# Reversing the queries of a tile in a sparse-attention trunk, so that the relative bias is read from a table of 24 KB

## The chip, the cores and the metric

The kernel runs on one core of one Trainium2 chip. The metric is device time in microseconds (us) of one execution; the time of a kernel is the median of its runs. The core has five engines with queues of their own: TensorE (PE in the profile; its weight loads are PEld), VectorE (DVE), ScalarE (ACT), GpSimd (POOL) and SyncE (SP). SP, ACT and POOL can issue DMAs, which 16 DMA engines carry out.

## The reference, cut to what matters

Two layers work on 256 tokens of width 2048. The first layer projects the normed input into a recurrence branch and an attention branch. The attention has 16 query heads and 4 key heads of width 128, and an indexer that scores every (query, key) pair and leaves 64 keys per query. What the change touches is this part:

```python
def block(bi):                      # 128 queries at a time
    s_h = jax.nn.relu(jnp.einsum('bqhd,bsd->bqhs', iqb, ik))
    score = jnp.einsum('bqhs,bqh->bqs', s_h, iwb) * idx_scale
    score = jnp.where(admissible[None], score, -jnp.inf)   # key < limit(query), chunks of 64
    _, sel = lax.top_k(score, topk)
    ...
    logits = jnp.einsum('bqgrd,bqkgd->bqgrk', qg, kg) * att_scale
    bias = rel_table[t5_bucket(sel - q_pos[None, :, None])]   # depends on key - query alone
    probs = jax.nn.softmax(logits + bias, axis=-1)
    o = jnp.einsum('bqgrk,bqkgd->bqgrd', probs, vg)
```

The bias of a head is a function of key position minus query position. Everything else (norms, gates, recurrence, the second layer's gated MLP, the embedding that is added after each layer) is matrix products with large weights, and elementwise work between them.

## The kernel before, in words

**The weight stream.** All large weights are float32 in HBM. They come as chunks of 128 x 1024 numbers (512 KB; the indexer's are 128 x 736) in one long list, `self.chunks`. For each chunk SP loads `raw` (13 buffers; L147), ACT rounds it to `hi` (L155), DVE subtracts to get `lo` (L156), and PE multiplies `hi` by the high and the low part of the activations and `lo` by the high part (three fp32r matmuls of 512 columns each: L189 to L191 into `pg`, or L229 to L231 into `Z`, `V`, `U`). Splits run three chunks ahead of their matmuls, loads up to five more ahead of the splits. Some chunks are made by adding a second weight block onto a used `raw` with a DMA that POOL issues (L160).

**Background tasks.** Everything else is generators (`idx_task`, `q_task`, `head_pair`, ...). After each chunk's matmuls the main loop takes one step of each live generator, so that a `yield` means about one chunk. A scheduler then puts the instructions of each engine into their final order; each engine runs its own list in that order, and waits where an operand is not there yet.

**The bias before.** `bias_table` computes a 16 x 384 table `bt` (head by key minus query) with one matmul (L487). An ACT-issued DMA (L493) then writes 128 copies of each head's row into the HBM tile `bias_d`, copy q shifted by q elements. For each pair of heads a POOL-issued DMA (L695) reads `bias`, a 128 x 2 x 256 tile whose row for query q is a piece of copy q.

**The attention before.** The transposes on PE have the data as weights and `ident` as the moving operand: of `iq` (L443, tile `iqt`), of `q` (L443, tile `qt`), and of the exponentials `L` (L735, tile `pt`). `head_pair` makes `bm` = bias + mask on POOL (L702, L703), the logits `lg` on PE (L706, L707), `L` = lg * rq + bm on DVE (L717) with its row maximum (L719), the exponentials and their sums `sm` on ACT (L725), then the reciprocal of the sums on DVE (L729, L731), the transposes `pt`, their copy `PT` on ACT (L737), the products with v (L744 to L746), and the scaled output `yb` on DVE (L754). `rq`, the norm of the queries, comes from the sums of squares `ss` (L630) by L675 on DVE and a power on POOL (L676). There are 8 head pairs, 4 query groups and 4 indexer steps.

**DMA lanes.** The DMAs that SP and ACT issue take eight completion semaphores in turn; an issue waits until the DMA that last had its semaphore has landed.

Of the kernel before, what the change touches and what calls it, by code (L numbers as in the profile page):

```python
# [27 lines left out]
T = 256  # L28
# [3 lines left out]
H = 16  # L32
# [49 lines left out]
class Trunk:  # L82
# [351 lines left out]
            nc.vector.tensor_tensor(lo, src, hi.bitcast(F32), op=OP.subtract)  # L434
        return hi, lo

    def fm(self, a0, a1, name="fm"):

        pt = self.pa(name)
        with self.tc.issue_after(self.last_mm.ins):  # L440
            for k in range(2):
                for t, x in ((0, a0), (1, a1)):
                    self.nc.tensor.transpose(pt[:, k * T + t * 128:k * T + (t + 1) * 128],  # L443
                                             x[:, k * 128:(k + 1) * 128], self.ident)
        return pt.rearrange("p (a b) -> p a b", a=2)

    def rms(self, ss, key):
# [18 lines left out]
    def consts(self):  # L466
        nc, a = self.nc, self.a
        self.cols = self.kept([128, C_ALL], "cols")
        nc.sync.dma_start(self.cols, a["cols"])
        self.ident = self.kept([128, 128], "ident")  # L470
        nc.gpsimd.dma_start(self.ident, a["ident"])
        self.mhalf = self.kept([128, 8], "mhalf")
        nc.gpsimd.memset(self.mhalf, -0.5)
        warm = self.kept([128, 8], "warm")
        nc.scalar.activation(warm, self.mhalf, AF.Tanh)
        self.r = {}

    def bias_table(self):
        nc, a = self.nc, self.a
        rel = self.kept([32, H], "rel")  # L480
        nc.gpsimd.dma_start(rel, a["rel_bias"])
        oh = self.kept([32, N_BUCKET_COLS], "oh")
        nc.gpsimd.dma_start(oh, a["onehot"])
# [4 lines left out]
        sb = self.kept([H, N_BUCKET_COLS], "bt")  # L488
        nc.scalar.activation(sb, ps[:H, :N_BUCKET_COLS], AF.Copy)

        bd = self.bias_d = self.dram.tile([H, 128, 512], F32, name="bias_d")
        yield
        nc.scalar.dma_start(bass.AP(tensor=bd.tensor, offset=bd.offset, ap=[[128 * 512, H], [513, 128], [1, 383]]),  # L493
                            sb[:, None, :383].to_broadcast([H, 128, 383]))
        self.done.add("bias")

    def lru_params(self):
# [28 lines left out]
    def idx_task(self, i, ps):  # L526

        nc = self.nc
        cp = lambda o, x: nc.scalar.activation(o, x, AF.Copy)
        if i == 0:  # L530
            self.iq = [[self.t(name="iq") for _ in range(2)] for _ in range(2)]
            self.iw = self.kept([128, 2, IH], "iw")
            self.score = self.t([128, 384], name="score")
            ikd = [self.t([128, 128], name="ikd") for _ in range(2)]
            for t in range(2):
                cp(ikd[t][:, 0:64], ps[t][:, 0:64])
                nc.vector.tensor_scalar(self.iw[:, t], ps[t][:, 64:80], IDX_SCALE, None, op0=OP.mult)
# [24 lines left out]
        yield  # L562

    def iq_task(self, j):

        nc = self.nc
        yield from self.until(f"iq{j // 2}")
        o = (j % 2) * T
        pt = self.fm(self.iq[j // 2][0][:, o:o + T], self.iq[j // 2][1][:, o:o + T], "iqt")
        iq = self.t([128, 2, T], name="iqT")  # L570
        nc.scalar.activation(iq, pt, AF.Copy)
        yield
        rl = []
        for step in range(3):
            for h, r in rl:
                hh = j * 4 + h
                for (c0, c1, t) in ((0, 256, 1), (256, 384, 0)):
                    w = self.iw[:, t, hh:hh + 1]
                    if hh == 0:
                        nc.vector.tensor_scalar(self.score[:, c0:c1], r[:, c0:c1], w, None, op0=OP.mult)  # L580
                    else:
                        nc.vector.scalar_tensor_tensor(self.score[:, c0:c1], r[:, c0:c1], w,
                                                       self.score[:, c0:c1], op0=OP.mult, op1=OP.add)
            rl = []
            if step < 2:
                ps = [self.pa("sc") for _ in range(2)]
                for c0, c1, q0 in ((0, 256, 128), (256, 384, 0)):
                    for b in (0, 64):
                        nc.tensor.matmul(ps[b // 64][:, c0:c1], iq[b:b + 64, step, q0:q0 + 128],
                                         self.ik[b:b + 64, 0:c1 - c0], start=True, stop=True)  # L590
                for i in range(2):
                    r = self.t([128, 384], name="rl")
                    nc.scalar.activation(r, ps[i][:, :384], AF.Relu)
                    rl.append((2 * step + i, r))
            if step == 1 and j < 3:
                self.spawn(self.iq_task(j + 1))
            yield 2
        if j == 3:
            yield from self.topk()

    def topk(self):
        nc = self.nc
        sc = self.score
        nc.vector.memset(sc[0:64, 192:256], OUT_OF_RANGE)
        nc.vector.memset(sc[0:64, 320:384], OUT_OF_RANGE)
        for rnd in range(8):
            for c0, c1 in ((0, 256), (256, 384)):
                m8 = self.sm([128, 8])
# [59 lines left out]
    def q_task(self, g, ps):  # L668
# [7 lines left out]
        nc.gpsimd.tensor_tensor(self.flat(rq), self.flat(rq), self.mhalf, op=OP.pow)  # L676
        self.rq[g] = rq
        qT = []
        for p in range(2):
            pt = self.fm(qs[0][:, p * T:(p + 1) * T], qs[1][:, p * T:(p + 1) * T], "qt")  # L680
# [3 lines left out]
        yield  # L684
        yield from self.until("mask", "k", "v", "bias")
        for p in range(2):
            self.spawn(self.head_pair(g, p, qT[p]), 0)
# [2 lines left out]
    def head_pair(self, g, p, qT):  # L690
# [39 lines left out]
        for i, t in ((0, 1), (1, 0)):  # L730
            nc.vector.tensor_scalar(rc[:, 2 * i:2 * i + 2], rc[:, 2 * i:2 * i + 2], self.rth("x", t), None, op0=OP.mult)  # L731
        for h in range(2):
            pt = self.pa("pt")
            for o, c in ((0, 256), (128, 0), (256, 128)):
                nc.tensor.transpose(pt[:, o:o + 128], L[h][:, c:c + 128], self.ident)  # L735
            x = self.t([128, 384], name="PT")
            nc.scalar.activation(x, pt[:, :384], AF.Copy)  # L737
            PT.append(x)
        yield
        po = self.pa("o")  # L740
        kv = slice(g * 128, (g + 1) * 128)
# [500 lines left out]
def _layout(i):  # L1242
# [28 lines left out]
    def plain(key, w):  # L1271
# [35 lines left out]
        "ident": np.eye(128, dtype=np.float32),  # L1307
        "onehot": _buckets(),
    }

# [14 lines left out]
```

## Time and profile before

| | us |
|---|---|
| median of 3 runs (1245.07 to 1247.82) | 1246.75 |
| the profiled execution, its own time | 1248.01 |
| its span from first to last instruction | 1246.2 |
| PE busy, share of the span | 1227.4 (98%) |
| DVE busy | 944.3 (76%) |
| ACT busy | 785.0 (63%) |
| POOL busy | 147.4 (12%) |

The profiled execution took 1.26 us more than the median, and 1.8 us of its time lie outside the span. A matmul's record includes its way through the array, so that records overlap: the time a matmul costs the stream is the distance of its start to the next one's, which the chain view gives directly.

### The profile page before, as it was taken

How to read it: one execution, taken by the hardware profiler on the slowest of the kernel's cores; microseconds unless marked ns; L12 is line 12 of the kernel's file. 1: busy time of each engine (PE TensorE's matmuls, PEld its weight loads, DVE VectorE, ACT ScalarE, POOL GpSimd, SP SyncE). 2: the span in 40 equal slices, each digit the busy share in tenths (PEclk: the TensorE clock that was granted, in tenths of full speed). 3: DMA queues.
4: the chain of work that ended last, by engine and by line, in shares of the span. 5: the costliest groups of instructions: out<-in, count | busy, mean ns of one | idle time of the engine just before them, and what ended most of it. 6: DMA issues, size and time to landing. Idle time of an engine off the chain costs nothing.

```text
span 1246.2 us, 16543 instructions
## 1 busy us (share of the span) xinstructions
PE 1227.4 (98%) x5780; PEld 1023.8 (82%) x5780; DVE 944.3 (76%) x1487; ACT 785.0 (63%) x1099; POOL 147.4 (12%) x178
## 2 busy tenths in 40 slices
PE   7999999999999999999999999999999999999998
PEld 7978887888888888888888888788888888887886
DVE  6779658786677778775568877887899778677865
ACT  6755546664477878863466776676765656565753
POOL 0001131412000001000110110032112000100100
PEclk9999999999999999999999999999999999999999
DMA  9997997636546555576787798889999965986961
GB/s 345 253 249 231 299 219 240 227 128 199 183 157 201 172 186 177 178 239 216 188 246 250 187 291 281 225 241 271 274 274 277 279 222 156 244 267 203 261 186 43
DMA packets 82868, 279.31 MB, mean 224 GB/s; under 512 B 9264, under 2 KB 11968, under 8 KB 82784
## 3 DMA queue, kind: packets, MB, share of 16 engines
q1 hardware_dynamic: 66672, 225.18, 52.0%
q0 software_dynamic: 14048, 49.94, 21.2%
q10 hardware_dynamic: 2064, 3.14, 1.9%
q8 instruction: 45, 0.74, 0.2%
q14 instruction: 39, 0.32, 0.1%
HBM read 270.89 MB, written 7.33 MB: 223 GB/s over the span
## 4 chain that ended last, share of the span: by engine, by line
PE 89%; DMA 5%; DVE 3%; issue 2%; ACT 1%; SPq 0%; POOL 0%; DVEq 0%; ACTq 0%
PE pg L191 22%; PE pg L189 22%; PE pg L190 22%; DMA bias_d<-bt 3%; PE U L229 1%; PE U L231 1%; PE U L230 1%; DVE lo L156 1%; ACT hi L155 1%; PE ht L443 1%; PE Z L230 1%; PE Z L229 1%; PE Z L231 1%; PE V L230 1%; PE U L290 1%
## 5 line engine op out<-in xcount | busy, mean ns | idle before, releaser
L156 DVE TENSOR_TENSOR lo<-raw,hi 128x1024 fp32r<-128x1024 f32 (+1 forms) x492 | 587.6, 1212 | 201.5 <-ACT hi L155 197.2
L155 ACT ACTIVATE hi<-raw 128x1024 fp32r<-128x1024 f32 (+1 forms) x492 | 511.5, 1048 | 350.2 <-PE pg L191 256.0
L189 PE MATMUL pg<-hi,xh 128*128 128x512 f32 (+1 forms) x1376 | 536.9, 390 | 6.8 <-ACT xh L426 6.3
L190 PE MATMUL pg<-lo,xh 128*128 128x512 f32 (+1 forms) x1376 | 532.0, 387 | 0.5 <-DVE lo L156 0.5
L191 PE MATMUL pg<-hi,xl 128*128 128x512 f32 (+1 forms) x1376 | 531.9, 387 | 0.5 <-DVE xl L427 0.4
L189 PEld LDWEIGHTS pg<-hi,xh 128*128 128x128 f32 x1376 | 259.5, 189 | 57.6 <-ACT xh L426 6.9
L191 PEld LDWEIGHTS pg<-hi,xl 128*128 128x128 f32 x1376 | 259.0, 188 | 51.7 <-DVE xl L427 1.6
L190 PEld LDWEIGHTS pg<-lo,xh 128*128 128x128 f32 x1376 | 259.5, 189 | 49.1 <-DVE lo L156 1.0
L160 POOL DMA_DIRECT2D raw<-in_w7h x32 | 27.7, 866 | 357.3 <-DMA raw<-in_w 197.5
L160 POOL DMA_DIRECT2D raw<-in_w x48 | 41.8, 892 | 203.7 <-DVE lo L156 110.6
L426 ACT ACTIVATE xh<-ht,cols 128x256 fp32r<-128x256 f32 x48 | 22.0, 469 | 19.1 <-DVE xl L427 11.9
L803 POOL TENSOR_TENSOR tt<-tt,tg 128x512 f32<-128x512 f32 x8 | 10.3, 1294 | 183.1 <-ACT tt L801 164.3
L229 PE MATMUL U<-hi,xh 128*128 128x512 f32 x72 | 29.0, 403 | 0.0
L231 PE MATMUL U<-lo,xh 128*128 128x512 f32 x72 | 28.1, 390 | 0.0
L230 PE MATMUL U<-hi,xl 128*128 128x512 f32 x72 | 28.1, 390 | 0.0
L427 DVE SCALAR_TENSOR_TENSOR xl<-ht,cols,xh 128x256 fp32r<-128x256 f32 x48 | 22.6, 481 | 5.7 <-ACT xh L426 5.6
L725 ACT ACTIVATE L<-L,s 128x256 f32<-128x256 f32 (+1 forms) x32 | 14.3, 448 | 15.5 <-DVE s L719 14.8
L434 DVE TENSOR_TENSOR xl<-s,xh 128x512 fp32r<-128x512 f32 x32 | 22.0, 687 | 1.9 <-ACT xh L433 1.9
L433 ACT ACTIVATE xh<-s 128x512 fp32r<-128x512 f32 x32 | 19.9, 622 | 4.8 <-DVE s L414 4.7
L717 DVE SCALAR_TENSOR_TENSOR L<-lg,rq,bm 128x256 f32<-128x256 f32 (+1 forms) x32 | 12.0, 410 | 14.4 <-POOL bm L702 12.4
L829 DVE SCALAR_TENSOR_TENSOR xc<-xat,cols,xc 128x255 f32<-128x255 f32 (+2 forms) x48 | 22.2, 477 | 0.5
L231 PE MATMUL V<-lo,xh 128*128 128x512 f32 x48 | 18.8, 391 | 0.5 <-DVE lo L156 0.5
(310 smaller groups left out, 1346.9 us busy)
## 6 DMA issues: line engine op xcount, KB each, us to landing
raw<-in_w SPq DMA_DIRECT2D x356, 512.0 KB, 5.0
raw<-in_w POOLq DMA_DIRECT2D x48, 512.0 KB, 8.7
raw<-in_w7h POOLq DMA_DIRECT2D x32, 512.0 KB, 7.1
raw<-in_w7h SPq DMA_DIRECT2D x24, 512.0 KB, 4.4
raw<-in_idx_w SPq DMA_DIRECT2D x24, 368.0 KB, 7.4
raw<-in_pe_w SPq DMA_DIRECT2D x8, 512.0 KB, 6.0
bias_d<-bt ACTq DMA_DIRECT2D x1, 3064.0 KB, 35.9
x<-in_xT SPq DMA_DIRECT2D x8, 256.0 KB, 7.3
```

The costliest lines, as they stand in the source:

```text
L155: nc.scalar.activation(hi[:, :c.cols], raw, AF.Copy)
L156: self.last_lo = nc.vector.tensor_tensor(lo[:, :c.cols], raw, hi[:, :c.cols].bitcast(F32), op=OP.subtract)
L160: nc.gpsimd.dma_start(c.raw, c.next.ap, accum_op=OP.add)
L189: self.nc.tensor.matmul(ps, xh, wh, start=(c == order[0] and k == 0), stop=False)
L190: self.nc.tensor.matmul(ps, xh, wl, start=False, stop=False)
L191: self.last_mm = self.nc.tensor.matmul(ps, xl, wh, start=False, stop=(c == order[-1] and k == 1))
L229: nc.tensor.matmul(st[b], ah, wh, start=new and k == 0, stop=False, skip_group_check=True)
L230: nc.tensor.matmul(st[b], al, wh, start=False, stop=False, skip_group_check=True)
L231: self.last_mm = nc.tensor.matmul(st[b], ah, wl, start=False, stop=(c == order[3] and k == 1), skip_group_check=True)
L426: nc.scalar.activation(hi[:, s], src[:, s], AF.Copy, scale=g)
L427: nc.vector.scalar_tensor_tensor(lo[:, s], src[:, s], g, hi[:, s].bitcast(F32), op0=OP.mult, op1=OP.subtract)
L829: nc.vector.scalar_tensor_tensor(xc[:, s, k:], xa[:, s, :T - k], col(C_CW + (3 - k) * 16 + f), xc[:, s, k:], op0=OP.mult, op1=OP.add)
```

## The change

Within each tile of 128 queries, the queries are taken in reverse for the logits and the scores. The bias row of the query in partition i then starts i elements further on in the table than that of partition 0, so a read with a step of one element per partition takes it straight from `bt`. `bias_d` becomes that table (16 x 384 floats, 24 KB) and its write is one row per head. To reverse the queries, the transposes of `iq`, `q` and `L` become matmuls with `flip`, the reversed identity, as the moving operand (the one for `L` turns the order back). What is held per query in partitions is reversed by small matmuls with `flip` as weights: `iw` (128 x 32, once, then an ACT copy), `ss` (128 x 8, once per query group) and `sm` (128 x 4, once per head pair, into a free part of the second `pt`). The steps behind these follow them: `rq` is computed one step later, and the reciprocal reads `pt` after the transposes. The constant `ident` grows from 64 to 128 KB.

```diff
-    def fm(self, a0, a1, name="fm"):
+    def fm(self, a0, a1, name="fm", flip=False):
...
+                    if flip:
+                        self.nc.tensor.matmul(o, x, self.flip, start=True, stop=True)
+                    else:
+                        self.nc.tensor.transpose(o, x, self.ident)
...
-        bd = self.bias_d = self.dram.tile([H, 128, 512], F32, name="bias_d")
-        yield
-        nc.scalar.dma_start(bass.AP(tensor=bd.tensor, offset=bd.offset, ap=[[128 * 512, H], [513, 128], [1, 383]]),
-                            sb[:, None, :383].to_broadcast([H, 128, 383]))
+        self.bias_d = self.dram.tile([H, N_BUCKET_COLS], F32, name="bias_d")
+        yield
+        nc.scalar.dma_start(self.bias_d, sb)
...
+                nc.tensor.matmul(pt[:, T:T + 2 * IH], self.flip, self.flat(self.iw), start=True, stop=True)
+            self.iw = self.kept([128, 2, IH], "iwf")
+            nc.scalar.activation(self.flat(self.iw), pt[:, T:T + 2 * IH], AF.Copy)
...
-        rq = self.kept([128, 2, 4], "rq")
-        nc.vector.tensor_scalar(rq, ss, 128 * EPS, None, op0=OP.add)
...
+        ps = self.pa("rq")
+        with self.tc.issue_after(self.last_mm.ins):
+            nc.tensor.matmul(ps[:, 0:8], self.flip, self.flat(ss), start=True, stop=True)
+        rq = self.kept([128, 2, 4], "rq")
+        nc.vector.tensor_scalar(self.flat(rq), ps[:, 0:8], 128 * EPS, None, op0=OP.add)
...
-        nc.gpsimd.dma_start(bt, bass.AP(tensor=bd.tensor, offset=bd.offset + h0 * 128 * 512 + 127,
-                                        ap=[[512, 128], [128 * 512, 2], [1, T]]))
+        nc.gpsimd.dma_start(bt, bass.AP(tensor=bd.tensor, offset=bd.offset + h0 * N_BUCKET_COLS,
+                                        ap=[[1, 128], [N_BUCKET_COLS, 2], [1, T]]))
...
-        rc = self.sm([128, 4])
-        nc.vector.reciprocal(rc, sm)
...
-                nc.tensor.transpose(pt[:, o:o + 128], L[h][:, c:c + 128], self.ident)
+                nc.tensor.matmul(pt[:, o:o + 128], L[h][:, c:c + 128], self.flip, start=True, stop=True)
+            if h == 1:
+                nc.tensor.matmul(pt[:, 384:388], self.flip, sm, start=True, stop=True)
...
+        rc = self.sm([128, 4])
+        nc.vector.reciprocal(rc, pt[:, 384:388])
```

SP's list keeps its order. On DVE the reciprocal of a head pair moves behind several splits (`lo`). This is the first pair; `s_1725` and `s_1730` are its sums `sm`. Before:

```order
L717 SCALAR_TENSOR_TENSOR L_1743<-lg_1689,rq_1599,bm_1686 128x128
L719 TENSOR_REDUCE s_1724<-L_1743 128x1
L156 TENSOR_TENSOR lo_1751<-raw_1221,hi_1750 128x1024
L729 RECIPROCAL s_1802<-s_1725 128x4
L731 TENSOR_SCALAR s_1802<-s_1802,rx_466 128x2 x2
L156 TENSOR_TENSOR lo_1774<-raw_1661,hi_1773 128x1024
```

With the change, on DVE at the same place:

```order
L156 TENSOR_TENSOR lo_1756<-raw_1224,hi_1755 128x1024
L156 TENSOR_TENSOR lo_1779<-raw_1666,hi_1778 128x1024
L156 TENSOR_TENSOR lo_1791<-raw_1697,hi_1790 128x1024
L156 TENSOR_TENSOR lo_1829<-raw_1710,hi_1828 128x1024
L156 TENSOR_TENSOR lo_1860<-raw_1736,hi_1859 128x1024
L749 RECIPROCAL s_1820<-pt_1813 128x4
L751 TENSOR_SCALAR s_1820<-s_1820,rx_466 128x2 x2
```

The reciprocal stands four splits later, and its operand is now a PSUM bank that PE fills.

On PE, a query group gets its small matmul 18 rows (one and a half chunks) behind its eight `qt` blocks. These are the last blocks of the chunk ahead of it, with the change; before, the L691 row is not there:

```order
L190 MATMUL pg_1634<-lo_1561,xh_117 128x512
L191 MATMUL pg_1634<-hi_1560,xl_118 128x512
L691 MATMUL rq_1647<-s_1592,ident_79 128x8
L229 MATMUL Z_1307<-hi_1582,xh_165 128x512
L230 MATMUL Z_1307<-hi_1582,xl_166 128x512
```

`flip` is a part of the tile `ident`, so both print as `ident`. The 128-column blocks `iqt`, `qt` and `pt` stand where they stood, as matmuls.

## Rows read from the trace of the kernel before

**Rows 1.** The page: busy time by engine, and PE in 40 slices.

```profile
PE 1227.4 (98%) x5780; PEld 1023.8 (82%) x5780; DVE 944.3 (76%) x1487; ACT 785.0 (63%) x1099; POOL 147.4 (12%) x178
PE   7999999999999999999999999999999999999998
```

**Rows 2.** Stretches: length, busy of PE, PEld, DVE, ACT, POOL; clock, DMA share, GB/s.

```profile
70.00:80.00 10.00, 10.00 (x52) 7.70 (x51) 1.93 (x3) 2.03 (x4) 0.00 (x0) 1.00 0.73 166
80.00:90.00 10.00, 7.59 (x40) 5.93 (x39) 9.87 (x23) 7.91 (x15) 0.00 (x0) 1.00 1.01 392
```

**Rows 3.** The chain that ended last, 14 to 110 us: start, us, what.

```profile
38.97 35.94 DMA bias_d<-bt
74.98 3.58 DMA raw<-in_w
78.66 1.06 ACT hi L155
```

**Rows 4.** Waits of SP's queue, 30 to 110 us: total, times, longest.

```profile
SPq L147 <- DMA bias_d<-bt: 33.0, 1, 33.0
```

**Rows 5.** Timeline of PE at its longest stop: start, us, what, idle before.

```profile
87.71 0.92 PE L589 MATMUL sc<-ik,iqT 64*128 64x256 f32 x8 [2.41 <-ACT iqT L571]
```

**Rows 6.** Groups of PE by line and form: records, busy us, mean ns.

```profile
L735 PE MATMUL pt<-ident,L 128*128 128x128 f32 x48 | 6.5, 272 | 0.0
L744 PE MATMUL o<-v,PT 128*128 128x128 f32 x32 | 6.3, 277 | 0.4 <-ACT PT L737 0.4
...
L443 PE MATMUL qt<-ident,q 128*128 128x128 f32 x24 | 3.1, 272 | 0.0
L443 PE MATMUL iqt<-ident,iq 128*128 128x128 f32 x16 | 2.4, 272 | 0.0
...
L443 PE MATMUL qt<-ident,c 128*128 128x128 f32 x8 | 1.0, 272 | 0.0
```

**Rows 7.** The chain over the whole span: one group of transposes, one of matmuls.

```profile
153.45 0.87 PE qt L443 x8
...
948.41 0.89 PE mix L1057 x8
```

**Rows 8.** Timeline of PE around the one matmul of the bias table.

```profile
37.03 0.81 PE L487 MATMUL bt<-oh,rel 32*16 32x384 f32 x2
37.77 0.43 PE L189 MATMUL pg<-hi,xh 128*128 128x368 f32 x1
38.05 0.33 PE L190 MATMUL pg<-lo,xh 128*128 128x368 f32 x1
38.21 0.33 PE L191 MATMUL pg<-hi,xl 128*128 128x368 f32 x1
```

**Rows 9.** Timeline of DVE: the sums of squares of the first query group are done.

```profile
156.61 0.17 DVE L675 TENSOR_SCALAR rq<-s 128x8 f32<-128x8 f32 x1
```

**Rows 10.** Timelines of DVE and PE, third head pair's reciprocal and transposes.

```profile
238.15 0.17 DVE L729 RECIPROCAL s<-s 128x4 f32<-128x4 f32 x1
...
242.32 0.82 PE L735 MATMUL pt<-ident,L 128*128 128x128 f32 x6
```

**Rows 11.** Timelines of DVE, POOL and PE, first and second head pair.

```profile
166.33 0.48 DVE L717 SCALAR_TENSOR_TENSOR L<-lg,rq,bm 128x256 f32<-128x256 f32 x1 [4.42 <-POOL bm L702]
...
187.48 0.74 POOL L702 TENSOR_TENSOR bm<-bias,mb 128x256 f32<-128x256 f32 x1 [7.81 <-DMA bias<-bias_d]
...
188.26 0.77 DVE L717 SCALAR_TENSOR_TENSOR L<-lg,rq,bm 128x256 f32<-128x256 f32 x2 [7.98 <-POOL bm L702]
...
193.81 0.50 PE L231 MATMUL V<-lo,xh 128*128 128x512 f32 x1 [0.53 <-DVE lo L156]
...
196.72 0.49 PE L744 MATMUL o<-v,PT 128*128 128x128 f32 x2 [0.38 <-ACT PT L737]
```

**Rows 12.** Line L695, the eight loads of bias: issue to landing.

```profile
DMA to landing us min/median/max: 3.0/4.9/11.0
```

**Rows 13.** Line L1000, eight loads of one 2 KB row into 128 partitions.

```profile
DMA to landing us min/median/max: 6.4/8.3/11.7
```

More of the change, by code (lines that the diff above doesn't have):

```diff
@@ L442, in fm @@
                 for t, x in ((0, a0), (1, a1)):
-                    self.nc.tensor.transpose(pt[:, k * T + t * 128:k * T + (t + 1) * 128],
-                                             x[:, k * 128:(k + 1) * 128], self.ident)
+                    o = pt[:, k * T + t * 128:k * T + (t + 1) * 128]
+                    x = x[:, k * 128:(k + 1) * 128]
+                    if flip:
+                        self.nc.tensor.matmul(o, x, self.flip, start=True, stop=True)
+                    else:
+                        self.nc.tensor.transpose(o, x, self.ident)
         return pt.rearrange("p (a b) -> p a b", a=2)
@@ L469, in consts @@
         nc.sync.dma_start(self.cols, a["cols"])
-        self.ident = self.kept([128, 128], "ident")
-        nc.gpsimd.dma_start(self.ident, a["ident"])
+        both = self.kept([128, 256], "ident")
+        nc.gpsimd.dma_start(both, a["ident"])
+        self.ident, self.flip = both[:, 0:128], both[:, 128:256]
         self.mhalf = self.kept([128, 8], "mhalf")
@@ L487, in bias_table @@
             nc.tensor.matmul(ps[:H, :N_BUCKET_COLS], rel, oh, start=True, stop=True)
-        sb = self.kept([H, N_BUCKET_COLS], "bt")
+        sb = self.t([H, N_BUCKET_COLS], name="bt")
         nc.scalar.activation(sb, ps[:H, :N_BUCKET_COLS], AF.Copy)
-        bd = self.bias_d = self.dram.tile([H, 128, 512], F32, name="bias_d")
+        self.bias_d = self.dram.tile([H, N_BUCKET_COLS], F32, name="bias_d")
         yield
-        nc.scalar.dma_start(bass.AP(tensor=bd.tensor, offset=bd.offset, ap=[[128 * 512, H], [513, 128], [1, 383]]),
-                            sb[:, None, :383].to_broadcast([H, 128, 383]))
+        nc.scalar.dma_start(self.bias_d, sb)
         self.done.add("bias")
@@ L568, in iq_task @@
         o = (j % 2) * T
-        pt = self.fm(self.iq[j // 2][0][:, o:o + T], self.iq[j // 2][1][:, o:o + T], "iqt")
+        pt = self.fm(self.iq[j // 2][0][:, o:o + T], self.iq[j // 2][1][:, o:o + T], "iqt", True)
         iq = self.t([128, 2, T], name="iqT")
@@ L603, in topk @@
         sc = self.score
-        nc.vector.memset(sc[0:64, 192:256], OUT_OF_RANGE)
-        nc.vector.memset(sc[0:64, 320:384], OUT_OF_RANGE)
+        nc.vector.memset(sc[64:128, 192:256], OUT_OF_RANGE)
+        nc.vector.memset(sc[64:128, 320:384], OUT_OF_RANGE)
         for rnd in range(8):
@@ L673, in q_task @@
         self.head_sums(qs, ss)
-        rq = self.kept([128, 2, 4], "rq")
-        nc.vector.tensor_scalar(rq, ss, 128 * EPS, None, op0=OP.add)
-        nc.gpsimd.tensor_tensor(self.flat(rq), self.flat(rq), self.mhalf, op=OP.pow)
-        self.rq[g] = rq
         qT = []
         for p in range(2):
-            pt = self.fm(qs[0][:, p * T:(p + 1) * T], qs[1][:, p * T:(p + 1) * T], "qt")
+            pt = self.fm(qs[0][:, p * T:(p + 1) * T], qs[1][:, p * T:(p + 1) * T], "qt", True)
             x = self.t([128, 2, T], name="qT")
@@ L684, in q_task @@
         yield
+        ps = self.pa("rq")
[3 more added lines that the diff above has]
+        nc.vector.tensor_scalar(self.flat(rq), ps[:, 0:8], 128 * EPS, None, op0=OP.add)
+        nc.gpsimd.tensor_tensor(self.flat(rq), self.flat(rq), self.mhalf, op=OP.pow)
+        self.rq[g] = rq
         yield from self.until("mask", "k", "v", "bias")
@@ L727, in head_pair @@
         yield
-        rc = self.sm([128, 4])
-        nc.vector.reciprocal(rc, sm)
-        for i, t in ((0, 1), (1, 0)):
-            nc.vector.tensor_scalar(rc[:, 2 * i:2 * i + 2], rc[:, 2 * i:2 * i + 2], self.rth("x", t), None, op0=OP.mult)
         for h in range(2):
@@ L738, in head_pair @@
             PT.append(x)
+        rc = self.sm([128, 4])
+        nc.vector.reciprocal(rc, pt[:, 384:388])
+        for i, t in ((0, 1), (1, 0)):
+            nc.vector.tensor_scalar(rc[:, 2 * i:2 * i + 2], rc[:, 2 * i:2 * i + 2], self.rth("x", t), None, op0=OP.mult)
         yield
@@ L1306, in _layout @@
         "pT": c(np.asarray(i["p"])[:, 0].reshape(2, T, 2, 128).transpose(0, 3, 2, 1)),
-        "ident": np.eye(128, dtype=np.float32),
+        "ident": np.concatenate([np.eye(128, dtype=np.float32), np.eye(128, dtype=np.float32)[::-1]], axis=1),
         "onehot": _buckets(),
```

## The prediction

> **What bounds the kernel now.** The page comes first: PE is busy for 98% of the span, DVE for 76%, ACT for 63% and POOL for 12% [rows 1]. In the 40 slices PE has a 7 at the start, an 8 at the end, and nines between them [rows 1]. So the kernel's time is the length of PE's list of instructions plus the few places where PE stops. What another engine gains or loses counts only if it starts or ends such a stop, and what PE's own list gains or loses counts in full.
>
> The second view is a table of stretches, to find those places. Between 80 and 90 us PE is busy for 7.59 of 10 us at a granted clock of 1.00, and just before, from 70 to 80 us, DVE and ACT work for only 2 us each [rows 2]. The chain says why: the write of the shifted copies starts at 38.97 us and takes 35.94 us; the weight load behind it is issued at 74.98 us, and its rounding starts on ACT at 78.66 us [rows 3]. The queue's own waits name the mechanism: SP stood for 33.0 us, once, for the landing of `bias_d` [rows 4]. The load did not need the data; its completion semaphore was the one that the write still held. SP is in order, so all loads behind it stood too. The 13 `raw` buffers carried PE until about 85 us; then PE was idle for 2.41 us [rows 5].
>
> **The change, part by part.** *The write.* 3064 KB become 24 KB, one row for each of 16 heads. SP's order is the same and a load will again share a semaphore with this write, but a write that lands within a few us doesn't use up a lead of 13 buffers. DVE and ACT, which stood for most of 70 to 80 us, get that time as well, but PE was fed for all but the 2.41 us, so that I credit no more. The price is -2.4 us; it can't be much more, and less only if something else takes the place of this stop.
>
> *The 96 blocks.* There are 4 x 4 blocks of `iqt`, 4 x 8 of `qt` and 8 x 6 of `pt`, 96 in all, and each turns from a transpose into a float32 matmul. The forms of PE show what that means. The 16, 24 + 8 and 48 transposes have as many records [rows 6]. The products `o` at L744, of which there are 16 (one for each head), have 32 [rows 6]: a float32 matmul goes through PE twice. What one pass takes of the stream is in the chain: eight transposes 0.87 us, 0.109 each; the eight records of four 128-column float32 matmuls (`mix`) 0.89 us, 0.111 each [rows 7]. A block so goes from 0.109 to 0.222 us, and 96 x 0.1135 = 10.9 us. Nothing hides that: it lies in PE's own list, within the 98%. It would be free only where PE stands anyway, and of such time the attention stretch has hardly any (below).
>
> *The 13 small matmuls* (1 of 32 columns, 4 of 8, 8 of 4). No row shows one so narrow. Two passes and two weight loads cost more than nothing, and hardly more than a 128-column float32 matmul, 0.22 us. The nearest row is the lone matmul of the bias table: from its start at 37.03 us to where the next 368-column matmul would have to have started (38.05 less 0.16, the step from 38.05 to 38.21) are 0.86 us [rows 8]. Its 2 x 384 columns take 0.65 us at the 0.85 ns a column of the transposes (0.87 us over 1024) [rows 7], so that 0.2 us are fixed cost. I take 0.2 us for each, 2.6 us together; the ends are 0 and 2.9 us. The Trainium skill (TensorE: Matmul & The Clock Gate, section "Wait — 56ns, not 53.3ns?") has start-to-start never below about 25 ns however narrow a matmul is; as an estimate from that page 26 passes would take 0.65 us and the kernel come to 1256 us, and no run here shows it.
>
> *Does PE wait for their operands?* The matmul for `rq` stands 18 matmuls of 512 columns behind the `qt` blocks. In the first group these started at 153.45 us [rows 7]; with 8 x 0.22 us for them and at least 18 x 0.16 us behind [rows 8] PE is there at 158.1 us or later, and DVE had the sums at 156.61 us [rows 9]. So no wait. The one for `sm` follows matmuls that need the same exponentials. The power on POOL comes a step later, in front of a `head_pair` that uses it two steps after; POOL is 12% busy [rows 1]. The extra ACT copy (128 x 32) and the moved reciprocals lie on engines with a quarter of their time free; if that cover were gone, the copy would cost less than the 1.06 us of a rounding of 1024 columns [rows 3].
>
> *The constant.* 64 KB more at the start, where PE waits for the first chunk; at the 392 GB/s of a full stretch [rows 2] 0.2 us at most, which I take.
>
> **The sum.** -2.4 + 10.9 + 2.6 + 0.2 = +11.3 us. The profiled execution's own time is 1248.0 us (span 1246.2 and 1.8 around it), so 1259.3 us in its terms. It was 1.26 us slower than the median of the runs shown, which gives **1258 us** as the median with the change. The gain is a stop that PE mostly slept through on its buffers; the price is paid in the one engine that has no time.
>
> **The rivals.**
>
> *A: no change.* The reversed identity is streamed like the identity, and a `flip` block goes through in one pass. Then 10.9 us fall away and +0.4 remain: 1247 us. It decides from an added cost below 0.02 us a block. What speaks against it is that one pass or two follows the kind of instruction in every group of the trace [rows 6], and `mix`, with the same 128 x 128 operands, pays two [rows 7]. 5 in 100.
>
> *B: bias loads that land later.* All 256 rows of a load now come from the same 3 KB of HBM; before they lay 2 KB apart. The nearest rows are the loads of one 2 KB row into 128 partitions, median 8.3 us [rows 13], against 4.9 us for `bias` now [rows 12]: 3.4 us more. What a late load does is seen in the first two head pairs: POOL waits for `bias`, DVE for POOL. In the first pair DVE stood 4.42 us and PE didn't notice; in the second 7.98 us, and PE was idle for 0.53 + 0.38 = 0.9 us [rows 11]. With 3.4 us more, the first pair's stop becomes as long as the second's, 0.9 us, and the second's grows by the whole 3.4: 4.3 us more, 1262 us. Against it: the single-row loads ran in a later and fuller stretch, and other pairs have room of some 4 us. 15 in 100. The Trainium skill (DMA: Bandwidth & Descriptors, section "Latency and other measured facts") reports that copies whose partitions are a large power of two apart in HBM lose up to half their rate, and supposes that the streams hit the same channels; it speaks of pitches of 512 KiB and up, so that a pitch of one element is my extension. By it landings would double to 9.8 us, the same arithmetic gives some 7 us, and the time would be 1265 us; no run shows it yet.
>
> *C: DVE stands at the reciprocal.* It now waits for PE, and behind it in DVE's list stand splits that PE will need. In the third pair DVE did it at 238.15 us, and PE came to the transposes only at 242.32 us [rows 10]: at that place DVE would stand for over 4 us. The scheduler has moved it behind more splits (four in the first pair), so that PE has three to five chunks in hand when DVE stands, and the copy on ACT that feeds the next product already waits for the same transposes. If every one of the eight cost what the second pair's stop costs, 0.9 us, 7.2 us come on top: 1265 us. It would have to be a stop of about 8 us to cost PE anything, by the two pairs of rows 11. 10 in 100.
>
> **How the numbers follow.** The forecast holds 70 in 100, A 5, B 15, C 10. The likeliest case, 1258 us, is the prediction. With small matmuls at nothing and the second pair's 0.9 us gone it is 1254.4 us; A lies outside. Upwards B is at 1262 and C at 1265 us, and with the small matmuls at 2.9 us a little more. The range is 1253.5 to 1266 us. About 0.2% (2.5 us) is what a measurement of this kernel can tell from no change. Slower by more than that holds for the forecast, B and C: 0.95. Within it lies most of A: 0.04. Faster would take A with free small matmuls and the 0.9 us gone: 0.01.
>
> **What would show it.** In the profile with the change: no wait of SP for `bias_d`, DVE and ACT busy from 70 to 80 us, and no stop of PE at 85 us (first step); twice the records for `iqt`, `qt` and `pt`, and some 1.77 us for eight `qt` blocks in the chain (second); about 0.2 us around each `rq` matmul (third); PE still at 98%, with PE's busy time up by 13 to 14 us. A shows as 48 records of `pt` and 0.11 us a block; B as landings of `bias` near 8 us and a longer wait of POOL at `bm`; C as DVE's wait for PE at the reciprocal followed by PE's waits for `lo`. I am wrong if PE's added passes are hidden in stops that I don't see, or if PE has new stops of several us between 150 and 345 us.

## The result and the profile after

The changed kernel takes 1257.94 us (median of 4 runs, 1257.17 to 1258.98), the kernel before 1246.45 us on the same chip: ratio 1.0093, 95% interval 1.0075 to 1.0110. The forecast was 1258 us. The profiled execution took 1257.22 us, its span 1255.4 us, 9.2 us over the one of before.

The page of the changed kernel, its PE row and the row of the queue that carries the write (packets, MB, share); before, the write had 2064 packets and 3.14 MB:

```profile
PE 1239.4 (99%) x5902; PEld 1037.7 (83%) x5902; DVE 942.5 (75%) x1487; ACT 785.4 (63%) x1100; POOL 144.5 (12%) x178
...
q10 hardware_dynamic: 32, 0.02, 0.0%
```

Stretches of the changed kernel (columns as in [rows 2]), and SP's wait for the table:

```profile
70.00:80.00 10.00, 10.00 (x53) 8.12 (x52) 8.16 (x21) 5.86 (x9) 0.00 (x0) 1.00 0.53 162
80.00:90.00 10.00, 10.00 (x56) 7.83 (x55) 7.15 (x14) 6.34 (x11) 0.00 (x0) 1.00 0.51 159
180.00:200.00 20.00, 20.00 (x111) 17.36 (x110) 11.01 (x20) 10.42 (x19) 5.62 (x8) 1.00 0.72 174
```
```profile
SPq L147 <- DMA bias_d<-bt: 2.4, 1, 2.4
```

The stop at 87.7 us is gone, SP's 33.0 us [rows 4] are 2.4, DVE and ACT work from 70 to 80 us, and PE works through the second head pair's stretch, where it had stopped for 0.9 us [rows 11].

The groups of PE by form in the changed kernel, and two links of its chain; they answer to [rows 6, 7]:

```profile
L742 PE MATMUL pt<-ident,L 128*128 128x128 f32 x96 | 12.0, 274 | 0.0
...
L447 PE MATMUL qt<-ident,q 128*128 128x128 f32 x48 | 5.8, 275 | 0.0
L447 PE MATMUL iqt<-ident,iq 128*128 128x128 f32 x32 | 4.2, 274 | 0.0
L744 PE MATMUL pt<-s,ident 128*128 128x4 f32 x16 | 2.3, 212 | 0.0
L447 PE MATMUL qt<-ident,c 128*128 128x128 f32 x16 | 1.9, 275 | 0.0
L691 PE MATMUL rq<-s,ident 128*128 128x8 f32 x8 | 1.1, 213 | 0.0
```
```profile
153.53 1.78 PE qt L447 x16
177.34 1.34 PE pt L742 x12
```

Twice the records, and 1.78 us for eight blocks, 1.34 for six: 0.223 us a block, where it was 0.109. The records' mean (274 ns) hardly differs from that of the transposes (272 ns), since records overlap; what a block costs is read from start to start.

Timeline of PE in the changed kernel, the stop that nobody had foreseen (1.10 us idle, at the transposed index key), and a small product in the stream:

```profile
43.31 0.33 PE L191 MATMUL pg<-hi,xl 128*128 128x368 f32 x1
44.73 0.33 PE L554 MATMUL ikt<-ident,ikd 128*128 128x128 f32 x1 [1.10 <-DVE ikd L548]
...
159.25 0.28 PE L691 MATMUL rq<-s,ident 128*128 128x8 f32 x2
159.39 0.48 PE L229 MATMUL Z<-hi,xh 128*128 128x512 f32 x1
159.70 0.39 PE L230 MATMUL Z<-hi,xl 128*128 128x512 f32 x1
159.93 0.40 PE L231 MATMUL Z<-lo,xh 128*128 128x512 f32 x1
```

From the start of the `rq` product to the second product behind it are 0.45 us; one of those products takes 0.23 us from start to start, so the eight columns cost 0.22 us. The two passes are not what costs: in the single records of the trace the second starts 25 to 31 ns behind the first, in each of the small products. The rest lies between the passes and the next products: 0.11 us until `Z` starts, and 0.31 us instead of 0.23 from there to the one behind it.

**A ruler.** Everything that the change touches lies behind the product of the bias table and ahead of the `gate` products of the recurrence. The ruler ends at one of these, which has a stop in front of it in every run; to the very first `gate` product the lengths differ by the same 10.7 us. The two starts, of the kernel before and then of the changed one, give a length that the later stops (DVE's `hr`, up to 2 us each, different from run to run) don't blur:

```profile
37.03 0.81 PE L487 MATMUL bt<-oh,rel 32*16 32x384 f32 x2
...
506.43 0.39 PE L842 MATMUL gate<-xl,xh 128*128 128x256 f32 x1 [0.74 <-DVE xl L434]
```
```profile
36.57 0.81 PE L493 MATMUL bt<-oh,rel 32*16 32x384 f32 x2
...
516.65 0.38 PE L855 MATMUL gate<-xl,xh 128*128 128x256 f32 x1 [0.71 <-DVE xl L434]
```

469.40 us before, 480.08 after: +10.7. Every run below was read with this ruler ("stage"), beside its time. A stage is read from one traced execution; of the two kernels that were traced twice, one differs by 0.2 us from trace to trace and the other (e5 and e12) by 0.85, so that less than about 1 us says nothing.

| run | time, us | ratio to before (95%) | stage, us | to before |
|---|---|---|---|---|
| before | | | 469.40 | |
| changed kernel; again beside e12 | 1257.94; 1258.07 | 1.0093 (1.0075 to 1.0110); 1.0089 (1.0076 to 1.0101) | 480.08; 479.85 | +10.7; +10.4 |
| e1 blocks only | 1252.64 | 1.0057 (1.0044 to 1.0069) | 474.93 | +5.5 |
| e2 flip by transpose | 1248.68 | 1.0026 (1.0016 to 1.0037) | 470.77 | +1.4 |
| e5; e12 no small products | 1252.80; 1253.22 | 1.0057 (1.0043 to 1.0071); 1.0048 (1.0036 to 1.0061) | 476.92; 476.07 | +7.5; +6.7 |
| e6 small table only | 1244.46 | 0.9986 (0.9975 to 0.9996) | 468.10 | -1.3 |
| e3 write on POOL | 1246.61 | 1.0006 (0.9996 to 1.0016) | 468.74 | -0.7 |
| e8 the same, order kept | 1243.71 | 0.9982 (0.9972 to 0.9993) | 464.99 | -4.4 |
| e7 iqT blocks only | 1244.81 | 0.9987 (0.9978 to 0.9996) | 466.98 | -2.4 |
| e10 write later | 1244.03 | 0.9980 (0.9971 to 0.9989) | 466.94 | -2.5 |
| e4 write put back | 1264.52 | 1.0152 (1.0138 to 1.0167) | 486.75 | +17.4 |
| e13 the same, own buffer | 1257.51 | 1.0095 (1.0078 to 1.0112) | 479.02 | +9.6 |

### The profile page after: what moved, and what is told of

Its sections match the earlier page's. It is cut to its first block, busy times and chain, and to the rows that moved or that the text cites. A ratio compares the mean times of both kernels' runs of the same rounds, so it can differ in the third digit from the quotient of the medians.

```text
span 1255.4 us, 16791 instructions
## 1 busy us (share of the span) xinstructions
PE 1239.4 (99%) x5902; PEld 1037.7 (83%) x5902; DVE 942.5 (75%) x1487; ACT 785.4 (63%) x1100; POOL 144.5 (12%) x178
## 4 chain that ended last, share of the span: by engine, by line
PE 94%; DVE 2%; DMA 2%; issue 0%; ACT 0%; SPq 0%; POOL 0%; DVEq 0%; ACTq 0%; POOLq 0%
PE pg L189 23%; PE pg L191 23%; PE pg L190 23%; DMA hr<-hd 1%; PE U L229 1%; PE U L230 1%; PE U L231 1%; DVE lo L156 1%; PE Z L229 1%; PE V L229 1%; PE ht L449 1%; PE Z L230 1%; PE V L230 1%; PE Z L231 1%; PE V L231 1%; PE pt L742 1%
## 5 line engine op out<-in xcount | busy, mean ns | idle before, releaser
L816 POOL TENSOR_TENSOR tt<-tt,tg 128x512 f32<-128x512 f32 x8 | 10.4, 1294 | 184.3 <-ACT tt L814 165.6
L728 DVE SCALAR_TENSOR_TENSOR L<-lg,rq,bm 128x256 f32<-128x256 f32 (+1 forms) x32 | 12.0, 407 | 13.6 <-POOL bm L713 11.4
L229 PE MATMUL Z<-hi,xh 128*128 128x512 f32 x48 | 18.9, 395 | 0.0
```

Of the source, the lines that this page charges most:

```text
L229: nc.tensor.matmul(st[b], ah, wh, start=new and k == 0, stop=False, skip_group_check=True)
```

## The experiments

Theory: the second pass of the 96 blocks is the price, the small products add to it, and the write gives back the stop that it made by SP's wait for its semaphore. Rivals: A of the prediction, and that the write costs through the bandwidth it takes.

**The blocks.** e1 puts a product with the plain identity into the kernel before:

```diff
...
-                nc.tensor.transpose(pt[:, o:o + 128], L[h][:, c:c + 128], self.ident)
+                nc.tensor.matmul(pt[:, o:o + 128], L[h][:, c:c + 128], self.ident, start=True, stop=True)
```

The blocks of `iqt` and `qt` are edited in the same way.

> The kernel before, with one part of the change alone: the 96 blocks of iqT, qT and P transposed by a 4-byte matrix product with the plain identity in place of the transpose operation; nothing is reversed, the 3 MB write and its reads stay, the output is the reference's. Theory (a 4-byte product costs TensorE twice a transpose, 0.22 against 0.11 us in its stream): the blocks read about 0.22 us each, +10.9 us on the kernel before, about 1257.5, and the stop of 2.4 us at 87.7 is still there. Rival A (the product with the identity costs one pass like the transpose): within 0.2% of the kernel before, the distances from block to block stay at 0.11 us.

e2 goes the other way: in the changed kernel the reversal stays, the second pass goes.

```diff
-                        self.nc.tensor.matmul(o, x, self.flip, start=True, stop=True)
+                        self.nc.tensor.transpose(o, x, self.flip)
...
-                nc.tensor.matmul(pt[:, o:o + 128], L[h][:, c:c + 128], self.flip, start=True, stop=True)
+                nc.tensor.transpose(pt[:, o:o + 128], L[h][:, c:c + 128], self.flip)
```

> The changed kernel, with the 96 blocks reversed by the transpose operation whose moving operand is the reversed identity, in place of the 4-byte product; the rest of the change stays. Theory (the second pass of the product is the price, and the transpose operation multiplies by whatever moving operand it is given): the blocks read 0.11 us each, -10.9 us on the changed kernel, about 1247, that is no change within 0.3% of the kernel before, because the 24 small products (+2.6) take what the write gives (-2.4). Rival (the price is not in the blocks but in what the reversal does around them, the small products and the new stop of 1.1 us at the index key): it stays within 2 us of the changed kernel, 1256 to 1258.

Links of the chain in e1, then in e2:

```profile
175.89 1.34 PE pt L739 x12
```
```profile
175.08 0.66 PE pt L742 x6
```

A product costs 0.223 us a block with the plain identity too, a transpose with the reversed one 0.110. So A falls, the reversal itself costs nothing, and the transpose does multiply by what it is given. The times differ by less than 10.9 us, though: e2 is 9.1 to 9.3 us of stage below the changed kernel, and e1 only 5.5 above the kernel before. In e1 SP stood as long as ever, but PE hardly stopped. Its rows (stretch; SP's wait; the write in its chain; timeline of PE at the score), and at the end PE's last product ahead of the score in the kernel before:

```profile
80.00:90.00 10.00, 9.90 (x51) 7.99 (x52) 9.87 (x24) 7.85 (x13) 0.00 (x0) 1.00 1.03 413
```
```profile
SPq L147 <- DMA bias_d<-bt: 33.4, 1, 33.4
```
```profile
38.72 34.97 DMA bias_d<-bt
```
```profile
86.13 0.39 PE L191 MATMUL pg<-hi,xl 128*128 128x512 f32 x1
86.61 0.92 PE L593 MATMUL sc<-ik,iqT 64*128 64x256 f32 x8
```
```profile
84.91 0.39 PE L191 MATMUL pg<-hi,xl 128*128 128x512 f32 x1
```

PE came to the score 1.2 us later than in the kernel before (86.13 against 84.91 for the product ahead of it), and the write had landed 1.2 us earlier (73.69 against 74.92 us): the 2.41 us were gone. I had expected the stop to stay. New theory: work on PE ahead of a late operand is paid out of the stop. e7 tests it with the 16 blocks of `iqt` alone (the same edit, for `iqt` only):

> The kernel before with only the 16 blocks of iqT as 4-byte products with the plain identity; the 3 MB write stays, and so does the output. Theory (more work on TensorE ahead of a late operand is paid out of the stop): 12 of these blocks lie ahead of the score at 87.7, 0.115 us each, so that its stop falls from 2.4 to 1.0 us or less, and of +1.8 us for the blocks at most 0.5 is left on the time. Rival (work and stop add up): the stop stays at 2.2 us or more, 1.8 us more than the kernel before.

PE is busy for 9.98 us between 80 and 90 us, and with more work on the engine that bounds the kernel it was not slower but 0.13% faster (0.04 to 0.22), so the rival falls.

The traces divide the stop between the work and the landing. The score starts 12.8 us after the write has landed in the kernel before, 12.9 in e1 and 12.8 in e7: the landing sets when its operand is there. The landing came 1.2 and 1.1 us earlier in e1 and e7, and PE came to the score 1.2 and 1.35 us later. So about half of the 2.41 us was paid by the added work, as the theory has it, and half by an earlier landing, for which the edits give no reason; the write took 35.0 to 36.0 us in the five runs of this shape (before, e1, e7, e10, e13). With the landing of the kernel before, e1 would still have stopped for some 1.2 us, by this count. That e7 got faster is more than the theory gives: of 1.8 us, 1.35 are paid back. The second head pair's stop is gone in this run too (PE busy for 19.96 of the 20 us from 180 us on), and why is not shown.

**The small products.** e5 (and e12 once more, beside the changed kernel) takes them out. There are 13 of them with 26 records; the 24 in the expectations is my miscount.

```diff
-                nc.tensor.matmul(pt[:, T:T + 2 * IH], self.flip, self.flat(self.iw), start=True, stop=True)
...
-            nc.tensor.matmul(ps[:, 0:8], self.flip, self.flat(ss), start=True, stop=True)
...
-                nc.tensor.matmul(pt[:, 384:388], self.flip, sm, start=True, stop=True)
```

> The changed kernel without the 24 small products (indexer weights, query sums and sums of the exponentials are used unreversed: this part of the computation is left out). The 96 reversed blocks and the small table stay. Theory (each stands 0.1 us or more in TensorE's stream, 2.6 us together, and the stop of 1.1 us at the index key stays, since it comes from the order on VectorE): 2 to 3 us less than the changed kernel, about 1255.3, with the stop at the index key still 1.0 to 1.3 us. Rival 1 (they stand where TensorE would wait anyway): no change within 1 us. Rival 2 (the product on the indexer weights makes the stop at the index key): 3.5 to 4 us less, about 1254, the stop gone.

> The changed kernel as it is, beside the next run on one chip, for the price of the small products: 1256.5 to 1259.

> The changed kernel without its 24 small products once more (the indexer weights, the query sums and the sums of the exponentials are used unreversed), beside the changed kernel on one chip. Theory (they cost their 0.1 us and more each in TensorE's stream and nothing besides): 2.0 to 3.2 us less than the changed kernel. Rival (some of them also make TensorE or VectorE wait where no stop is seen): 4 us less or more.

Stage -3.2 and -3.8 us; time -4.9 us in both, each against the kernel before on its own chip. The theories of e5 and e12 are missed by the times. 13 x 0.22 = 2.9 us are seen in the stream, the rest of the stage is 0.3 to 0.9 us, and 1 to 2 us more appear in the times alone (4.1 us between the traced executions of e11 and e12). The stop at the index key is 1.10 us in both, so the product on the indexer's weights doesn't make it. What the last 1 to 2 us are stays open; the rival of e12 has the times on its side, but no stop that would bear it out.

**The table and the write.** e6 is the table of 24 KB alone, read without any reversal (each query gets its mirror's bias):

```diff
+        nc.scalar.dma_start(self.bias_d, sb)
...
+                                        ap=[[1, 128], [N_BUCKET_COLS, 2], [1, T]]))
```

> The kernel before, with the table of 24 KB alone: it is written and read as in the changed kernel, and nothing is reversed, so that each query gets the bias of its mirror query in the tile (this part of the computation is changed). No block, product or matrix of the change is there. Theory (my term for the write): 2.4 us less than the kernel before, about 1244, the stop at 87.7 gone. Rival (the waits around the write are worth more than the one stop, bias loads and the first head pairs' stops too): 4 to 6 us less, 1240 to 1242.

-1.3 us of stage: the 2.4 us are gone and the stop of 1.1 us at the index key has come, with no product near it. The order changed instead: DVE has 20 splits (`lo`) ahead of the index key here and in the changed kernel, where the kernel before has 18. Why the scheduler orders them so is not shown; in e4, with the long write on ACT's queue, there are 20 as well. e3 shows it larger, with 21. There the kernel before keeps its 3 MB, but GpSimd issues them:

```diff
-        nc.scalar.dma_start(bass.AP(tensor=bd.tensor, offset=bd.offset, ap=[[128 * 512, H], [513, 128], [1, 383]]),
+        nc.gpsimd.dma_start(bass.AP(tensor=bd.tensor, offset=bd.offset, ap=[[128 * 512, H], [513, 128], [1, 383]]),
```

> The kernel before, with the 3 MB write of the shifted copies issued by GpSimd's queue instead of ScalarE's; bytes, copies and the reads of the bias stay, and so does the output. Theory (SyncE's queue stood 33 us because its next load shared a completion semaphore with the write, so that TensorE ran out of weights at 87.7): the wait of 33 us on bias_d is gone from SyncE's queue, the stop of 2.4 us with it, 1243 to 1246. Rival (the write's 3 MB take the DMA engines from the weights whoever issues it): SyncE waits less, but weights come late all the same between 40 and 80 us, a stop of 1.5 us or more stays before 90 us, and the time is that of the kernel before within 0.2%.

PE's timeline in e3; below it e8, which adds to e3 that DVE's splits from weight 18 on queue behind the index key:

```profile
46.48 0.33 PE L549 MATMUL ikt<-ident,ikd 128*128 128x128 f32 x1 [2.64 <-DVE ikd L543]
```
```diff
...
+            with self.tc.issue_after(self.first.ins):
+                self.last_lo = lo_op()
...
```

> The kernel before with the 3 MB write on GpSimd's queue, and the splits of the weights held behind the scaling of the index key on VectorE, so that VectorE's and TensorE's orders are those of the kernel before. Theory (the write on GpSimd frees SyncE's queue, and what it gave back in the run without this was the stop of 2.6 us at the index key, made by three splits that the scheduler had put ahead): neither stop is there, 2 to 3 us less than the kernel before, 1242.5 to 1244. Rival (TensorE is held by the weights, so that a stop removed here comes back at the next late weight): within 1 us of the kernel before, with stops of 1 us or more elsewhere before 110 us.

```profile
80.00:90.00 10.00, 10.00 (x50) 7.95 (x49) 8.50 (x23) 5.61 (x10) 0.00 (x0) 1.00 1.03 411
```

In e3 SP has no wait for `bias_d`, and three splits more ahead of the key cost 2.64 us; its time so stayed that of the kernel before, above the 1243 to 1246 that I expected. In e8 (18 splits again) neither stop is there, with the 3 MB moved all the same (they landed at 76.3 us). So the write's bytes cost PE nothing that is seen; its semaphore did. e8 beats both kernels.

How much the semaphore costs, e10 asks, by issuing the write behind the next rounding:

```diff
...
-        yield
-        nc.scalar.dma_start(bass.AP(tensor=bd.tensor, offset=bd.offset, ap=[[128 * 512, H], [513, 128], [1, 383]]),
-                            sb[:, None, :383].to_broadcast([H, 128, 383]))
+        yield 3
+        with self.tc.issue_after(self.last_hi.ins):
+            nc.scalar.dma_start(bass.AP(tensor=bd.tensor, offset=bd.offset, ap=[[128 * 512, H], [513, 128], [1, 383]]),
+                                sb[:, None, :383].to_broadcast([H, 128, 383]))
```

> The kernel before with the 3 MB write issued one weight rounding later on ScalarE's queue (after the next hi, some 3 us later); nothing else is edited, and the output stays. Theory (what the write costs is how much later than TensorE's need the first weights behind it come, so it grows with the time of its issue): the write is issued at 42 instead of 39 us and lands near 78; the stops between 70 and 100 us are 5 us or more in all instead of 2.4, and where a single one is 2.9 us or longer the granted clock falls to half behind it, as in the run with the write put back: 3 to 6 us more than the kernel before, 1249 to 1252. Rival (the write costs its 2.4 us wherever it is issued): within 1.2 us of the kernel before, stops of 2 to 3 us in all.

Both theories lost: it got 0.20% faster (0.11 to 0.29). The edit moved the write less in time than I had expected, to 39.80 us instead of 42, and it landed at 75.3, 0.4 us later than before; yet the score does not stop. SP's wait in e10, PE at the score, then SP's weight loads issued between 30 and 43 us, in the kernel before and in e10:

```profile
SPq L147 <- DMA bias_d<-bt: 33.2, 1, 33.2
```
```profile
85.45 0.92 PE L590 MATMUL sc<-ik,iqT 64*128 64x256 f32 x8
```
```profile
36.64 5.24 SPq L147 DMA_DIRECT2D raw<-in_w  x6
```
```profile
34.94 7.18 SPq L147 DMA_DIRECT2D raw<-in_w  x8
```

SP stands as long, but behind eight loads instead of six. The program says why. SP's list with what each issue waits for, in the kernel before and in e10 (the eight `DMAHW` semaphores go round over the issues of SP and ACT; the number left out is the write's):

```
40 L896 DMA xn_438<-in_x 128x512 [waits DMAHW7_49]
41 L896 DMA xn_440<-in_x 128x512 [waits DMAHW1_49]
...
48 L147 DMA raw_742<-in_w 128x1024 [waits DMAHW0_49,DVE_49]
```
```
42 L147 DMA raw_544<-in_w 128x1024 [waits DMAHW1_49,DVE_49]
43 L147 DMA raw_579<-in_w 128x1024 [waits DMAHW3_49,DVE_49]
...
50 L147 DMA raw_806<-in_w 128x1024 [waits DMAHW2_49,DVE_49]
```

The write comes two issues later in the round, so the load that inherits its semaphore comes two loads later. Twelve products of 0.23 us are 2.7 us of PE's work for each load; two of them are more than the stop. The score starts 10.2 us after the landing and has no stop; in the kernel before it stood until 12.8 us after it.

Put back into the changed kernel, the write should then cost by the same count. e4 did it badly:

```diff
+        bd = self.dram.tile([H, 128, 512], F32, name="big")
...
+        nc.scalar.dma_start(bass.AP(tensor=bd.tensor, offset=bd.offset, ap=[[128 * 512, H], [513, 128], [1, 383]]),
+                            sb[:, None, :383].to_broadcast([H, 128, 383]))
```

> The changed kernel with the 3 MB write of the shifted copies put back beside the small one, at its old place on ScalarE's queue; nothing reads it. Theory from the blocks-only run (TensorE's own extra work had already covered the stop that the write made): SyncE's queue stands 30 us or more on the big write again, but TensorE comes to the score of 85 us 1.3 us later than in the kernel before, the stop there is under 1 us, and the time is that of the changed kernel within 1.5 us, 1256.5 to 1259.5. Rival (my term as predicted, the write costs 2.4 us whatever else is done): the stop of 2.4 us is back, 1260 to 1261.

DVE's waits, PE's timeline and two stretches of e4:

```profile
DVE xl L434 <- DMA big<-bt: 8.4, 1, 8.4
```
```profile
89.27 0.39 PE L191 MATMUL pg<-hi,xl 128*128 128x512 f32 x1
92.61 0.92 PE L600 MATMUL sc<-ik,iqT 64*128 64x256 f32 x8 [2.95 <-ACT iqT L582]
...
94.51 0.63 PE L189 MATMUL pg<-hi,xh 128*128 128x512 f32 x1
94.94 0.63 PE L190 MATMUL pg<-lo,xh 128*128 128x512 f32 x1
```
```profile
90.00:92.00 2.00, 0.00 (x0) 0.00 (x0) 2.00 (x5) 2.00 (x5) 0.00 (x0) 1.00 1.05 418
94.00:96.00 2.00, 2.00 (x6) 1.53 (x5) 2.00 (x3) 1.72 (x4) 0.00 (x0) 0.50 0.80 311
```

In the changed kernel `bt` lies in the rotating buffers. The write reads it for 34.5 us, and a tile of DVE's that came to the same buffer waited 8.4 us: a new wait of my own making, so e4 says nothing of the write's old price. e13 gives `bt` a buffer of its own again (`self.kept`), moves the one-hot table into the rotating buffers for it, and is otherwise e4:

> The changed kernel with the 3 MB write put back behind the small one, this time with the table it reads in a buffer of its own (and the one-hot table in the rotating buffers instead), so that no tile of the rotating buffers waits for the write; nothing reads what it writes. By the program, 7 weight loads stand ahead of the one that takes over the write's semaphore (6 in the kernel before, 8 in the run with the write issued later), and three splits stand ahead of the index key on VectorE, as in the run with the write on GpSimd. Theory (the write costs what the count of loads ahead of the standing one leaves uncovered, and one load is 2.7 us of TensorE's work): SyncE's queue stands 30 us, VectorE does not wait for the write, no stop of 1 us or more between 70 and 100 us, the stop at the index key is 2.6 instead of 1.1 us: 1258 to 1261. Rival (the write costs 2.4 us wherever it stands, as I predicted): a stop of 2 us or more between 70 and 100 us, 1261 to 1263.

```profile
SPq L147 <- DMA big<-bt: 25.6, 1, 25.6
```
```profile
80.00:90.00 10.00, 10.00 (x53) 8.09 (x52) 8.35 (x18) 6.49 (x11) 0.00 (x0) 1.00 1.00 380
```

SP stands 25.6 us, behind seven loads, and PE doesn't stop, though the write landed when it did in the kernel before (74.98 us); the time is that of the changed kernel (intervals overlap almost fully). The stop at the index key, which I expected at 2.6 us, was absent; that half of the expectation failed, since DVE's list has 18 splits ahead of the key here, as in the kernel before, and not three more. So with the blocks and seven loads ahead, the 3 MB cost nothing that is seen. In the changed kernel's own order of DVE the write was not run without e4's fault.

## Why the prediction was right

*What bounds the kernel* held: PE's busy share went from 98 to 99%, and the stages follow PE's list and its stops, with some 1 to 2 us left over (e1: stops 3.5 us shorter, so +9.0 us of work where the list has +10.9).

*The 96 blocks, +10.9 us.* The price in the stream was exact (0.223 us a block, 0.222 predicted). The net price was 9.1 to 9.3 us by e2 and 5.5 by e1, because stops of PE went: the added work filled half of the one at 87.7 us in e1, and the second head pair's stops (1.1 us before, 0.8 in e2) are gone in e1 and in the changed kernel. These are gone in e8 too, which adds no work, so that it isn't shown that the blocks fill them. "Nothing hides that" was the wrong sentence.

*The write, -2.4 us.* The mechanism was right (e3, e8: no semaphore, no stop, whatever the bytes), and the stop went. Its price was over-read twice. The step said that it could be less "only if something else takes the place of this stop", and something did: two splits more ahead of the index key, 1.10 us, leave -1.3 (e6). DVE's order was there to be read before the result; only its reciprocals were looked at. And with the blocks and one load more ahead, the write costs nothing (e13). The step also had the 13 `raw` buffers as PE's lead; what counts is how many loads were issued ahead of the one with the write's semaphore, six of them (e10: eight, with the same 13 buffers, and no stop).

*The 13 small products, +2.6 us.* 0.22 us each in the stream, 2.9 us, the upper end that I had named; with what they do around them 3.2 to 3.8 us of stage, and about 5 us of time. This term was too small. The Trainium skill (TensorE: Matmul & The Clock Gate, section "Wait — 56ns, not 53.3ns?") has start-to-start never below about 25 ns; the trace agrees, with 25 to 31 ns between the two passes. But the 0.65 us that I had estimated from it leave out what a product costs where it meets the products around it, and that is most of its 0.22 us.

*No wait for their operands, and the constant, +0.2 us.* The first held for PE: no stop stands at `rq` or at the products behind the reciprocals. Of the constant nothing is seen: the bias table's product started 0.46 us earlier than before, not later, and from 36.4 to 37.2 us in all the traces.

*The sum.* +11.3 predicted, +11.5 in the medians, +10.7 on the ruler. By e2, e6 and e5/e12 the parts are 9.2 + 3.5 - 1.3 = 11.4; that they come to 0.8 us more than the whole on the ruler fits stops that several parts share, and lies within what a stage can tell. So the number was good because three errors of about 1 to 2 us cancelled: the blocks too dear by 1.7 us, the small products too cheap by 0.9, the write credited with 1.1 too much. Read by stops it is the same luck: PE's stops over 0.1 us on the ruler went from 4.2 to 1.8 us, the 2.4 that I had forecast, but as -2.4 at the score, -1.1 in the second head pair and +1.1 at the index key, and the last two I had not foreseen. Without its stops the stage grew by 13.1 us; PE's busy time over the whole span rose by 12.0 us, not by the 13 to 14 that I had named.

*Rivals.* A is refuted by the records and by e1. B: the loads of `bias` in the changed kernel land about as before [rows 12] (median 5.1 us in e11, the same kernel again), so its 3.4 us never came:

```profile
DMA to landing us min/median/max: 3.9/4.2/10.7
```

The pitch of one element so shows none of what I had extended from the Trainium skill (DMA: Bandwidth & Descriptors, section "Latency and other measured facts"). C: DVE's eight reciprocals waited 1.0 us in all, no stop of PE follows one, and between 150 and 345 us PE was without a pause.

## What to carry to other kernels

A stop of the bounding engine is not a fixed price: work added ahead of it, an operand that comes sooner and the count of transfers ahead of the late one are all paid out of the same stop, so removing a stop and adding work don't simply sum. Before a long transfer is shrunk, look at who waits for its completion semaphore: another place in the round (e10, 0.20%), or another queue with DVE's order held (e8, 0.18%), gave as much as removing 3 MB of writes did (e6, 0.14%; the intervals overlap), and left the arithmetic alone. The other queue by itself gave nothing (e3), since the order changed with it: after every edit, read the order of all engines, and not only of those that the edit is about. A reversal belongs into the operand of a transpose, where it costs one pass; as a float32 product it costs two.

## What the runs showed of the hardware

- A transpose on TensorE with the reversed identity as its moving operand reverses, at 0.110 us a block; as a float32 product the same takes 0.223 us.
- A float32 product of 4 or 8 columns among larger ones takes 0.22 us of the stream, as much as one of 128 columns, though its two passes start 25 to 31 ns apart.
- After 2.95 us without work (e4) TensorE worked about 1.4 us at full speed, then the granted clock read 0.50, the lower level of 1.2 GHz, and products started every 0.43 us instead of 0.23 until about 97.1 us. Behind the 2.41 us of the kernel before the row of 80 to 90 us reads 1.00 [rows 2], and behind the 2.64 us of e3 it read 1.00 too, from 46 to 54 us.
